# Decoder step: rotary rows of the cache pages by copies to a scratch and one load, instead of gathers

## The chip, the cores and the metric

The kernel runs on one core of a Trainium2 chip. The core has five engines with their own instruction queues: TensorE (PE, matrix products into PSUM), VectorE (DVE), ScalarE (ACT), GpSimd (POOL) and SyncE (SP, which issues DMAs). An engine works through its queue in order; what it needs from another engine or from a DMA it waits for by semaphores. The metric is the device time of one execution in microseconds, median over runs. Less is better.

## The reference, cut to what matters

One layer of a decoder serves 512 prompt rows and 8 samples of 8 new rows each with the same weights. Of the samples' attention this is the part that the change touches: each sample reads 32 cache pages of 128 rows by its page table; a page has latent rows (256 wide) and rotary key rows (32 wide).

```python
def scores(c, kr):
    return (jnp.einsum('bhtl,bkl->bhtk', q_abs, c.astype(f32))
            + jnp.einsum('bhtr,bkr->bhtk', q_r, kr.astype(f32))) * ATTN_SCALE
...
def step(carry, pid):
    m, l, acc = carry
    c = cache_kv_latent[layer, pid]
    kr = cache_k_rope[layer, pid]
    s = scores(c, kr)
    m_new = jnp.maximum(m, jnp.max(s, -1))
    corr = jnp.exp(m - m_new)
    p = jnp.exp(s - m_new[..., None])
    acc = acc * corr[..., None] + jnp.einsum('bhtk,bkl->bhtl', p, c.astype(f32))
    return (m_new, l * corr + jnp.sum(p, -1), acc), None
(m, l, acc), _ = lax.scan(step, (m, l, acc), page_table.T)
```

Around it stand a conditioning (six modulation terms per group of rows), one input projection, causal prompt attention over 8 heads, a short gated convolution, gates, output projection, layer norm, and a SwiGLU feed forward.

## The kernel before

All 576 rows are kept with channels on the partitions, in two halves of 288 columns. A product in full precision is three matmuls of a high and a low part (`mm3`, L117 to L119). A weight tile is loaded by SyncE into `wr` (L107), ScalarE makes the high part `wh` (L57) and VectorE the low part `wl` (L60); there are three `wr` tiles and three pairs of parts.

The program goes through these stages: conditioning and first input tiles; latent projections; the prompt's attention (`prompt_units`), with the convolution units (`fill_conv`, 12 tiles of 48 matmuls) and the rest of the conditioning (`fill_ada`, weights `wa`, two tiles in a ring, L196) as fillers between its parts; the samples' attention (`sample_units`), with gates and projections as fillers; output projection and first norm; feed forward; second norm.

A scheduler that works on a timeline of its own sets the order of each engine's queue from the program. Only on SyncE, and only in the first stage and in the samples' attention, does the order of the program stand (`manual_schedule`).

The samples' attention goes over 4 pairs of samples. For each pair there is one step on the new rows and eight units of four pages for both samples, 32 units in all. `load` fetches a unit two ahead of its use: SyncE reads eight page numbers from `ptab` (L563) into registers and issues eight page loads of 256 KB (L569, tiles `raw`, a ring of 7). GpSimd issues four indirect gathers (L573, tile `kr`, a ring of 3): partition p of a gather gets one row of 128 numbers of `in_krT_dram`, a row number standing in `idx`. So each sample's 32 rotary rows come to 64 partitions, every row twice. In `scores` ScalarE rounds `kr` to `krh` and VectorE makes `krx`, which holds high parts and low parts on different partitions (L625, with the factor `nm`, 0 or -1); two matmuls (L632) multiply it by the queries `qr` after eight on the latent rows (L630). `prepare` makes `qr`, block-diagonal over the two samples.

DMAs of SyncE carry one of eight semaphores in turn (DMAHW0 to DMAHW7 in the order below); one that takes a semaphore waits for the DMA that had it before.

Of the kernel before, what the change touches and what calls it, by code (L numbers as in the profile page):

```python
# [7 lines left out]
F32 = mybir.dt.float32  # L8
# [35 lines left out]
# column offsets of the per-channel vectors  # L44
# [3 lines left out]
def build(tc, a):  # L48
# [29 lines left out]
    psp = pool("psp", space=PSUM)  # L78

# [9 lines left out]
    # ---------------------------------------------------------------- base  # L89
# [6 lines left out]
    # weight stream: pool, ring of split tiles, columns of a tile  # L96
    wp = [pool("w", side="right"), 3, 512, 3]

    def wload(src, n=1024, hl=None, tag="", to=None, eng=None):
        """a weight tile and its exact split, as a list of (hi, lo) pieces of wp[2] columns"""  # L100
# [25 lines left out]
    def gpart(pss, piece, xss, c0, ks, n):  # L126
        """pss[i] += sum over k in ks of piece[:, k-th 128 columns from c0]^T xss[i][k], of n such k in all"""
        for ps, xs in zip(pss, xss):
            for i, k in enumerate(ks):
                c = slice(c0 + 128 * i, c0 + 128 * i + 128)  # L130
                mm3(ps[:, :HT], piece[0][:, c], piece[1][:, c], *xs[k], k == 0, k == n - 1)

    def gemm(pss, w, xss, k0=0):
        """pss[i] = sum over k of w[:, k0+k]^T xss[i][k]; an xs is the (hi, lo) pairs of one half"""
# [4 lines left out]
    def halves(t):  # L139
        """operands of a half-token tile [128, 2, K, HT]"""  # L140
        return [(t[:, 0, k], t[:, 1, k]) for k in range(t.shape[2])]
# [7 lines left out]
    def rsqrt(p, vv, out, table=True):  # L149
        """out = 1/sqrt(vv): exp(-ln/2), then one Newton step"""  # L150
# [15 lines left out]
    # right-hand stack: what outlives the attention phases  # L166
# [10 lines left out]
    idx = keep.tile([128, 4 * NPAGES], I32, name="idx")  # L177
    lane = keep.tile([128, 1], I32, name="lane")
# [7 lines left out]
    # ---------------------------------------------------------------- start: ada, h  # L186
# [31 lines left out]
    # weights of the conditioning, in part where results come later  # L218
# [5 lines left out]
    # a quarter of the conditioning gives a quarter of the modulated rows, and those a quarter of the first three tiles  # L224
# [48 lines left out]
    # ---------------------------------------------------------------- latent projections  # L273
    # on the right what the queries end with, on the left what the prompt's attention ends with
# [88 lines left out]
    # values of the prompt, token-major  # L363
# [9 lines left out]
    # new latent rows of the samples, token-major  # L373
# [8 lines left out]
    dma(out=idx, in_=a["pages_b"])  # L382
    dma(out=lane, in_=a["lane"])
    dma(out=ptab, in_=a["pages"])
    v.tensor_scalar(out=idx, in0=idx, scalar1=32, scalar2=None, op0=MULT)
    tt(idx, idx, lane.to_broadcast([128, 4 * NPAGES]), ADD)
# [4 lines left out]
    # ---------------------------------------------------------------- fillers  # L391
# [70 lines left out]

    def fill_ada():
        for u in range(2, 6):
            yield from ada_mm(u, CV, 2)

    # ---------------------------------------------------------------- prompt attention
    E2 = pool("e2", side="right")
    A2b = pool("a2b")
    # each head's rows of the samples, with the other half's rows zero  # L470
# [25 lines left out]
    def prompt_units():  # L496
        for pr in range(4):
# [32 lines left out]
            for kb in range(4):  # L530
# [9 lines left out]
                # the two heads' columns of the array work side by side  # L540
# [7 lines left out]
    # ---------------------------------------------------------------- sample attention  # L548
    ring = {"raw": (0, NRAW, 5), "kr": (0, 3, 2)}

    def ring_tile(name, shape, dt=F32):
        """the next tile of a ring whose last places are in the later pool"""
# [4 lines left out]
    def load(pa, gg):  # L557
        """GP pages of the two batches, and their rotary rows"""
        pages = {}
        if gg < 0:  # L560
            return pages
        i = pa * NG + gg
        _, vs = nc.values_load_multi_w_load_instructions(  # L563
            ptab[i:i + 1, :], engines=[mybir.EngineType.SP], min_val=0, max_val=n_pool - 1,
            skip_runtime_bounds_check_because="a page table holds indices of the pool")
# [4 lines left out]
        kr = pages["kr"] = ring_tile("kr", [128, GK])  # L570
        for j in range(GP):
            i = pa * NPAGES + GP * gg + j
            g.indirect_dma_start(kr[:, 128 * j:128 * j + 128], None, a["krT"],  # L573
                                 bass.IndirectOffsetOnAxis(ap=idx[:, i:i + 1], axis=0))
        return pages

    def prepare(wk):
        """the samples' queries against latent rows, and the rotary ones"""
# [5 lines left out]
        # rotary queries against [hi, lo] rows of the first batch, then of the second: block-diagonal  # L584
        qf_ = qr.rearrange("p i a e q -> p (i a) e q")
        zero = sel[:, :NS].unsqueeze(1).to_broadcast([128, 8, NS])
        act(qf_[64:128, :, 0], zero[64:128], scale=0.0)
        act(qf_[0:64, :, 1], zero[0:64], scale=0.0)
        ps = ps_sc()
        mm(ps, lhsT=sel, rhs=qsr, start=True, stop=True)  # L590
        for e in range(2):
            src = ps[64 * e:64 * e + 64].rearrange("p (h a e t) -> p e a h t", a=4, e=2, t=NT)[:, e]
            d = qr[64 * e:64 * e + 64].rearrange("p i a e (h t) -> p i e a h t", t=NT)[:, :, e]
# [12 lines left out]
    def sample_units(A3, qa, qr, pages):  # L606
# [6 lines left out]
        def scores(pa, gg, pages):  # L613
            """scores of the step's own rows (gg < 0) or of GP pages"""
# [6 lines left out]
            else:  # L621
                krh = A3.tile([128, GK], F32R, tag="krh", bufs=1, name="krh")
                kx = A3.tile([128, GK], F32R, tag="krx", bufs=2, name="krx")
                act(krh, pages["kr"])
                v.scalar_tensor_tensor(out=kx, in0=krh.bitcast(F32), scalar=nm, in1=pages["kr"], op0=MULT, op1=ADD)  # L625
            # the two batches' columns of the array work side by side
# [565 lines left out]
```

## Time and profile before

| | |
|---|---|
| median of three runs | 1139.51 us (1139.26 to 1141.25) |
| span of the profiled execution | 1174.0 us, granted TensorE clock 0.974 |
| TensorE busy | 1091.8 us, 93% |
| VectorE busy | 537.7 us, 46% |
| ScalarE busy | 431.7 us, 37% |
| GpSimd busy | 225.1 us, 19%; 122.7 us of it the 128 gathers |
| DMA of SyncE's queue | 180.42 MB |
| DMA of GpSimd's queue | 8.40 MB |

The profile is of one execution with the profiler on, whose span is 34.5 us longer than the median of the runs without it. Times in the profile's rows count from the start of that span. Busy time leaves out an engine's waits and, for SyncE, everything: issuing a DMA is not counted as busy, so SyncE is read from its waits and its timeline. A row of waits has the engine and line that waited, what ended the wait, the sum in us, how often, and the longest.

### The profile page before, as it was taken

To read this page: it belongs to the slowest core of one execution; us is meant where nothing else is said; L and a number is where in the kernel's file an instruction comes from. 1 tells how busy PE (TensorE), PEld (TensorE's weight loads), DVE (VectorE), ACT (ScalarE), POOL (GpSimd) and SP (SyncE) were. 2 spreads that over 40 slices of the span, in tenths; PEclk is the share of its full clock that TensorE was granted. 3 is DMA by queue.
4 is the path that set the end of the run, shared out by engine and by line. 5 is a ranking of instruction groups with operands and counts; after the bars stand their busy time and mean duration, and the time that the engine had idled before them with its cause. 6 is when DMAs were issued, how large, how long until landed. Compare 5 with 4: busy or idle time off the path is not lost.

```text
span 1174.0 us, 19868 instructions
## 1 busy us (share of the span) xinstructions
PE 1091.8 (93%) x7646; PEld 931.6 (79%) x7646; DVE 537.7 (46%) x1059; ACT 431.7 (37%) x859; POOL 225.1 (19%) x232
## 2 busy tenths in 40 slices
PE   6889999998798899989999889899999999999994
PEld 5878787785466466556569889899999999999994
DVE  3476354443132333332247787933233333355656
ACT  2474343435232522332346355332223222334433
POOL 1120000023442342441301421800000000001303
PEclk9999999999799998999999899999999999999998
DMA  9626354418389586696675423032222222455551
GB/s 366 209 96 204 122 185 141 140 46 311 106 294 321 170 300 214 220 310 244 203 239 172 159 73 108 3 107 91 90 72 79 100 75 72 118 178 150 157 181 54
DMA packets 84941, 190.07 MB, mean 162 GB/s; under 512 B 11600, under 2 KB 15568, under 8 KB 84848
## 3 DMA queue, kind: packets, MB, share of 16 engines
q1 hardware_dynamic: 80752, 180.42, 45.8%
q0 software_dynamic: 4096, 8.40, 2.3%
q8 instruction: 60, 0.98, 0.3%
q14 instruction: 33, 0.27, 0.1%
HBM read 185.72 MB, written 3.06 MB: 161 GB/s over the span
## 4 chain that ended last, share of the span: by engine, by line
PE 48%; DVE 7%; DMA 5%; issue 2%; ACT 1%; SPq 1%; POOL 0%; POOLq 0%; ACTq 0%; DVEq 0%
PE acc L117 10%; PE acc L118 9%; PE acc L119 9%; PE sc L117 4%; PE sc L119 4%; PE sc L118 4%; PE sc L630 3%; DMA wr<-in_w_ff_dram 3%; PE pv L661 3%; DVE xr L60 2%; DVE wl L60 2%; ACT wh L57 1%; PE sc L632 1%; SPq L569 1%; DMA raw<-in_page_dram 1%
## 5 line engine op out<-in xcount | busy, mean ns | idle before, releaser
L117 PE MATMUL acc<-h,wl 128*128 128x288 f32 x960 | 288.7, 302 | 14.1 <-DVE wl L60 8.5
L118 PE MATMUL acc<-h,wh 128*128 128x288 f32 x960 | 286.9, 299 | 2.0 <-DVE h L60 1.5
L119 PE MATMUL acc<-h,wh 128*128 128x288 f32 x960 | 284.7, 297 | 1.9 <-issue 1.9
L60 DVE TENSOR_TENSOR wl<-wr,wh 128x512 fp32r<-128x512 f32 (+1 forms) x186 | 178.7, 966 | 212.1 <-ACT wh L57 206.1
L57 ACT ACTIVATE wh<-wr 128x512 fp32r<-128x512 f32 (+2 forms) x196 | 156.6, 807 | 194.5 <-DMA wr<-in_w_ff_dram 58.7
L117 PEld LDWEIGHTS acc<-h,wl 128*128 128x128 f32 x960 | 181.5, 189 | 25.9 <-DVE wl L60 11.2
L118 PEld LDWEIGHTS acc<-h,wh 128*128 128x128 f32 x960 | 182.2, 190 | 7.3 <-issue 5.0
L119 PEld LDWEIGHTS acc<-h,wh 128*128 128x128 f32 x960 | 182.6, 190 | 3.1 <-issue 2.9
L573 POOL DMA_INDIRECT kr<-in_krT_dram,idx x128 | 122.7, 959 | 227.4 <-ACT krh L57 103.0
L117 PE MATMUL sc<-h,wl 128*128 128x288 f32 x336 | 99.9, 297 | 0.0
L118 PE MATMUL sc<-h,wh 128*128 128x288 f32 x336 | 99.4, 296 | 0.0
L119 PE MATMUL sc<-h,wh 128*128 128x288 f32 x336 | 99.1, 295 | 0.0
L630 PE MATMUL sc<-raw,qa 128*64 128x512 f32 x256 | 85.3, 634 | 3.2 <-DMA raw<-in_page_dram 1.8
L60 POOL TENSOR_TENSOR xr<-xr,h 128x288 f32<-128x288 f32 x16 | 17.2, 1098 | 366.1 <-ACT h L57 362.5
L117 PE MATMUL acc<-f,wl 128*128 128x288 f32 x288 | 85.9, 298 | 1.6 <-DVE wl L60 1.6
L118 PE MATMUL acc<-f,wh 128*128 128x288 f32 x288 | 84.9, 295 | 0.0
L119 PE MATMUL acc<-f,wh 128*128 128x288 f32 x288 | 84.7, 294 | 0.0
L661 PE MATMUL pv<-raw,pT 128*64 128x256 f32 x512 | 68.8, 401 | 12.5 <-ACT pT L57 6.3
L661 PEld LDWEIGHTS pv<-raw,pT 128*64 128x64 f32 x512 | 38.5, 143 | 37.7 <-issue 16.0
L119 PEld LDWEIGHTS sc<-h,wh 128*128 128x128 f32 x336 | 63.6, 189 | 0.0
L118 PEld LDWEIGHTS sc<-h,wh 128*128 128x128 f32 x336 | 63.3, 189 | 0.1
L117 PEld LDWEIGHTS sc<-h,wl 128*128 128x128 f32 x336 | 63.2, 188 | 0.1
(326 smaller groups left out, 1767.1 us busy)
## 6 DMA issues: line engine op xcount, KB each, us to landing
raw<-in_page_dram SPq DMA_DIRECT2D x256, 256.0 KB
wr<-in_w_ff_dram SPq DMA_DIRECT2D x76, 512.0 KB
wa<-in_w_ada_dram SPq DMA_DIRECT2D x40, 512.0 KB
wr<-in_w_in_dram SPq DMA_DIRECT2D x64, 256.0 KB
wr<-in_w_ff_dram SPq DMA_DIRECT2D x16, 384.0 KB
wr<-in_w_o_dram SPq DMA_DIRECT2D x18, 256.0 KB
wr<-in_w_oa_dram SPq DMA_DIRECT2D x16, 256.0 KB
x<-in_xT_dram SPq DMA_DIRECT2D x4, 576.0 KB
```

The source lines that it names most:

```text
L57: nc.scalar.activation(out=out, in_=in_, func=func, **kw)
L60: return (eng or v).tensor_tensor(out=out, in0=in0, in1=in1, op=op)
L117: mm(ps, lhsT=wl, rhs=xh, start=start, stop=False)
L118: mm(ps, lhsT=wh, rhs=xl, start=False, stop=False)
L119: mm(ps, lhsT=wh, rhs=xh, start=False, stop=stop)
L569: dma(out=raw[:, j], in_=a["page"][bass.ds(vs[GP * e + j], 1)].rearrange("a p d -> p (a d)"))
L573: g.indirect_dma_start(kr[:, 128 * j:128 * j + 128], None, a["krT"], bass.IndirectOffsetOnAxis(ap=idx[:, i:i + 1], axis=0))
L630: mm(ps[rows(e), :n], lhsT=qa[:, c, 2 * pa + e], rhs=rhs, start=c == 0, stop=False)
L632: mm(ps[:, :n], lhsT=qr[:, i, pa].rearrange("p e q -> p (e q)"), rhs=kx, start=False, stop=i == 0)
L661: mm(pv[rows(e), :KVL], lhsT=pT[:np_, j, e], rhs=rhs, start=j == 0, stop=j == nj - 1)
```

## The change

The 128 gathers go, with the tables `idx` and `lane` and the two VectorE instructions that made the row numbers. A scratch `krs` in HBM holds for each of the 32 units 64 rows of 512 numbers: the first sample's 32 rotary rows over four pages, then the second's. A third filler of the prompt's attention, `fill_kr`, writes it: for each unit SyncE reads eight page numbers and issues eight copies from HBM to HBM, each of 32 rows of 128 numbers (16 KB), three units to a convolution unit. In `load` one DMA of SyncE brings a unit's 64 x 512 numbers from the scratch, behind the eight page loads. In `scores` the parts are made by `split`: high parts on partitions 0 to 63, low parts on 64 to 127. `prepare` lays `qr` out to match, by quarters of 32 partitions in place of halves.

```diff
+    krs = pool("kd", space=bass.MemoryType.DRAM).tile([4 * NG, 64, GK], F32, name="krs")
...
+    def fill_kr():
+        for i in range(4 * NG):
+            vs = page_ids(i)
+            for e in range(2):
+                for j in range(GP):
+                    dma(out=krs[i, 32 * e:32 * e + 32, 128 * j:128 * j + 128],
+                        in_=a["krP"][bass.ds(vs[GP * e + j], 1)].rearrange("a r d -> (a r) d"))
+            yield 1
...
-        kr = pages["kr"] = ring_tile("kr", [128, GK])
-        for j in range(GP):
-            i = pa * NPAGES + GP * gg + j
-            g.indirect_dma_start(kr[:, 128 * j:128 * j + 128], None, a["krT"],
-                                 bass.IndirectOffsetOnAxis(ap=idx[:, i:i + 1], axis=0))
+        kr = pages["kr"] = ring_tile("kr", [64, GK])
+        dma(out=kr, in_=krs[i])
...
-        act(qf_[64:128, :, 0], zero[64:128], scale=0.0)
-        act(qf_[0:64, :, 1], zero[0:64], scale=0.0)
         ps = ps_sc()
         mm(ps, lhsT=sel, rhs=qsr, start=True, stop=True)
-        for e in range(2):
-            src = ps[64 * e:64 * e + 64].rearrange("p (h a e t) -> p e a h t", a=4, e=2, t=NT)[:, e]
-            d = qr[64 * e:64 * e + 64].rearrange("p i a e (h t) -> p i e a h t", t=NT)[:, :, e]
+        for r in range(4):
+            e, rr = r % 2, slice(32 * r, 32 * r + 32)
+            act(qf_[rr, :, 1 - e], zero[rr], scale=0.0)
+            src = ps[rr].rearrange("p (h a e t) -> p e a h t", a=4, e=2, t=NT)[:, e]
+            d = qr[rr].rearrange("p i a e (h t) -> p i e a h t", t=NT)[:, :, e]
             act(d[:, 0], src)
             tt(d[:, 1], src, d[:, 0].bitcast(F32), SUB)
...
-                krh = A3.tile([128, GK], F32R, tag="krh", bufs=1, name="krh")
                 kx = A3.tile([128, GK], F32R, tag="krx", bufs=2, name="krx")
-                act(krh, pages["kr"])
-                v.scalar_tensor_tensor(out=kx, in0=krh.bitcast(F32), scalar=nm, in1=pages["kr"], op0=MULT, op1=ADD)
+                split(pages["kr"], kx[0:64], kx[64:128])
...
     def fill_ca():
-        ad = fill_ada()
+        ad, kg = fill_ada(), fill_kr()
         for _ in fill_conv():
             for _ in range(3):
                 next(ad, None)
+                next(kg, None)
             yield 1
```

The change shifts the line numbers by a few: L107 is L108 after it, L196 is L195, L198 is L197, L569 is L578; the copies are L470, the load of `kr` is L580.

SyncE in the prompt's attention, before, near the last convolution units (`wr` are weights of the projections, `wa` of the conditioning):

```order
L107 DMA wr<-in_w_in_dram 128x512 [waits DMAHW7_49,DVE_49]
L196 DMA wa<-in_w_ada_dram 128x1024 [waits DMAHW3_49,PE_49]
L196 DMA wa<-in_w_ada_dram 128x1024 [waits DMAHW5_49,PE_49]
L107 DMA wr<-in_w_in_dram 128x512 [waits DMAHW2_49,DVE_49]
L107 DMA wr<-in_w_in_dram 128x512 [waits DMAHW4_49,DVE_49]
L196 DMA wa<-in_w_ada_dram 128x1024 [waits DMAHW7_49,PE_49]
```

The same queue with the change, one convolution unit. Each copy is a register instruction (ISA) and a DMA; of the eight behind a table read the first and the last are shown:

```order
L108 DMA wr<-in_w_in_dram 128x512 [waits DMAHW2_49,DVE_49]
L195 DMA wa<-in_w_ada_dram 128x1024 [waits DMAHW3_49,PE_49]
L460 TENSOR_LOAD ptab
L470 ISA
L470 DMA krs<-in_krP_dram 32x128 [waits DMAHW4_49]
...
L470 DMA krs<-in_krP_dram 32x128 [waits DMAHW3_49]
L195 DMA wa<-in_w_ada_dram 128x1024 [waits DMAHW4_49,PE_49]
...
L490 DMA wqr<-in_w_uq_dram 128x384 [waits DMAHW6_49]
L108 DMA wr<-in_w_in_dram 128x512 [waits DMAHW7_49,DVE_49]
```

Between two loads of the fillers now stand eight copies and a table read, from the latent projections on to the last convolution unit.

GpSimd before, at the change from the prompt's attention to the samples' (the copies `co` belong to the last convolution unit):

```order
L413 COPY co<-up 128x2 [waits DVE_49]
L414 COPY co<-up 128x16 [waits DVE_49]
L573 DMA kr<-in_krT_dram,idx 128x128 [waits PE_49]
L573 DMA kr<-in_krT_dram,idx 128x128 x3
...
L573 DMA kr<-in_krT_dram,idx 128x128 [waits DMASW4_49,DVE_49]
```

GpSimd with the change, from the same place:

```order
L408 COPY co<-up 128x2 [waits DVE_49]
L409 COPY co<-up 128x16 [waits DVE_49]
L802 TENSOR_SCALAR xr<-xr 128x1152 [waits DMAHW2_49,DMAHW4_49,SP_sequencer_49,DMAHW6_49,DVE_49,PE_49]
L802 TENSOR_SCALAR xr<-xr 128x1152 [waits DMAHW5_49]
L802 TENSOR_SCALAR xr<-xr 128x1152 [waits DMAHW6_49]
```

GpSimd has nothing in the samples' attention; its next work is the residual of the first norm. What it issued stands on SyncE now, the end of a unit's `load`:

```order
L578 DMA raw<-in_page_dram 128x512 [waits DMAHW7_49]
L578 ISA
L578 DMA raw<-in_page_dram 128x512 [waits DMAHW0_49]
L580 DMA kr<-krs 64x512 [waits DMAHW1_49]
L614 DMA smask<-in_smask_dram 128x256 [waits DMAHW2_49,DVE_49]
L108 DMA wr<-in_w_in_dram 128x512 [waits DMAHW3_49]
```

The load of `kr` is behind the unit's last page load and ahead of the next filler weights.

More of the change, by code (lines that the diff above doesn't have):

```diff
@@ L176, in build @@
     ptab = keep.tile([4 * NG, 2 * GP], I32, name="ptab")
-    idx = keep.tile([128, 4 * NPAGES], I32, name="idx")
-    lane = keep.tile([128, 1], I32, name="lane")
     sel = keep.tile([128, 128], F32, name="sel")
@@ L381, in build @@
         split(wukr, wukh[:, c], wukl[:, c], g)
-    dma(out=idx, in_=a["pages_b"])
-    dma(out=lane, in_=a["lane"])
     dma(out=ptab, in_=a["pages"])
-    v.tensor_scalar(out=idx, in0=idx, scalar1=32, scalar2=None, op0=MULT)
-    tt(idx, idx, lane.to_broadcast([128, 4 * NPAGES]), ADD)
     dma(out=mask, in_=a["mask"])
@@ L461, in fill_gates, with page_ids @@
         yield 1
+    def page_ids(i):
+        return nc.values_load_multi_w_load_instructions(
+            ptab[i:i + 1, :], engines=[mybir.EngineType.SP], min_val=0, max_val=n_pool - 1,
+            skip_runtime_bounds_check_because="a page table holds indices of the pool")[1]
+    def fill_kr():
[6 more added lines that the diff above has]
+            yield 1
     def fill_ada():
@@ L562, in load @@
         i = pa * NG + gg
-        _, vs = nc.values_load_multi_w_load_instructions(
-            ptab[i:i + 1, :], engines=[mybir.EngineType.SP], min_val=0, max_val=n_pool - 1,
-            skip_runtime_bounds_check_because="a page table holds indices of the pool")
+        vs = page_ids(i)
         for e in range(2):
@@ L740, in fill_ca @@
                 next(ad, None)
+                next(kg, None)
             yield 1
-        for _ in ad:
-            pass
+        for x in (ad, kg):
+            for _ in x:
+                pass
     def merge(s, f, nf, ns):
@@ L1136, in pack @@
     r["page"] = np.concatenate([ct, ck], 2)
-    r["krT"] = i["cache_k_rope"][0].transpose(0, 2, 1).reshape(-1, PAGE)
+    r["krP"] = i["cache_k_rope"][0].transpose(0, 2, 1)
     pt = i["page_table"]
     r["pages"] = pt.reshape(4, 2, NG, GP).transpose(0, 2, 1, 3).reshape(4 * NG, 2 * GP)
-    r["pages_b"] = np.repeat(pt.reshape(4, 2, NPAGES).transpose(1, 0, 2).reshape(2, -1), 64, 0)
-    r["lane"] = (np.arange(128, dtype=np.int32) % 32)[:, None]
     r["ident"] = np.eye(128, dtype=np.float32)
@@ L1145, in pack @@
     r["sel"] = (p[:, None] % 32 == p[None, :] % 32).astype(np.float32)
-    r["nm"] = np.where(p % 64 < 32, 0.0, -1.0).astype(np.float32)[:, None]
+    r["nm"] = np.where(p < 64, 0.0, -1.0).astype(np.float32)[:, None]
     r["qtab"], r["krtab"] = rope_consts()
```

## The prediction

> **What bounds the kernel now.** I read the stretches first: busy time of each engine between the span's start, the end of the input projections (88), the end of the prompt's attention (256), the start and the end of the samples' attention (300 and 640).
>
> ```profile
> core 0: us, PE busy (x) PEld busy (x) DVE busy (x) ACT busy (x) POOL busy (x), PEclk, DMA share, GB/s
> 60.00:88.00 28.00, 24.50 (x151) 20.76 (x150) 21.58 (x36) 20.31 (x38) 6.27 (x4) 0.94 0.30 98
> 88.00:256.00 168.00, 168.00 (x1212) 134.41 (x1212) 81.29 (x209) 64.04 (x161) 6.85 (x18) 1.00 0.43 145
> 256.00:300.00 44.00, 36.75 (x205) 25.48 (x204) 14.95 (x43) 18.98 (x48) 19.25 (x19) 0.92 0.64 222
> 300.00:640.00 340.00, 313.75 (x1939) 214.15 (x1938) 116.84 (x288) 120.24 (x263) 99.49 (x105) 0.96 0.69 234
> ```
>
> TensorE is the bound: from 88 to 256 it is busy 168.00 of 168 us, from 300 to 640 it is idle for 340 - 313.75 = 26 us. The copies go into the first of these stretches, the gathers leave the last. GpSimd's 99.49 us there are nearly all gathers, on an engine that has time. So the gathers can cost something only where a late one holds TensorE up; the copies cost something where SyncE feeds TensorE late. What SyncE does from 88 to 248 is next: its waits in that window, then the DMAs that it issued in it.
>
> ```profile
> SPq L196 <- PE acc L198: 55.4, 20, 9.0
> SPq L107 <- DVE wl L60: 31.9, 14, 9.3
> SPq L196 <- DMA wa<-in_w_ada_dram: 10.4, 5, 3.8
> SPq L479 <- DVE up L60: 8.1, 1, 8.1
> SPq L479 <- DVE wql L60: 5.6, 3, 2.9
> SPq L107 <- DVE up L60: 4.7, 1, 4.7
> ...
> SPq L479 <- DMA wqr<-in_w_uq_dram: 0.2, 1, 0.2
> ```
> ```profile
> wa<-in_w_ada_dram SPq DMA_DIRECT2D x29, 512.0 KB
> wr<-in_w_in_dram SPq DMA_DIRECT2D x23, 256.0 KB
> wqr<-in_w_uq_dram SPq DMA_DIRECT2D x7, 192.0 KB
> wr<-in_w_ukT_dram SPq DMA_DIRECT2D x2, 256.0 KB
> ```
>
> The six waits shown make 116.1 us and the five others of that answer 6.8, together 122.9 of 160 us. What is left, 37 us, is SyncE's own work for some 62 loads. So SyncE has 123 us to spare there, and that is the room for the copies.
>
> **The price of one copy on SyncE.** No row shows a copy from HBM to HBM, but what an issue costs SyncE is seen.
>
> ```profile
> L569 SPq DMA_DIRECT2D raw<-in_page_dram x256: 3/333/1441, 264.8 to 605.0; - x128
> L569 SPq MOVE raw<-in_page_dram x256: 2/29/723, 264.7 to 604.9; - x128
> L563 SPq TENSOR_LOAD <-ptab x32: 3/536/744, 245.4 to 592.9; - x32
> ```
> ```profile
> 29.17 0.33 SPq L383 DMA_DIRECT2D lane<-in_lane_dram  x1
> 264.82 9.14 SPq L569 DMA_DIRECT2D raw<-in_page_dram  x16
> ```
> ```profile
> raw<-in_page_dram SPq DMA_DIRECT2D x256, 256.0 KB
> ...
> lane<-in_lane_dram SPq DMA_DIRECT2D x1, 0.5 KB
> ```
>
> A page load of 256 KB takes 333 ns to issue, the half KB of `lane` 0.33 us: the size doesn't enter, so a copy of 16 KB costs the same. A copy is addressed through registers as a page load is (FUSED_REGOPS, MOVE, DMA), and 16 of those, with one read of the page table between them, take 9.14 us where nothing holds them up. One unit of eight copies with its table read (0.536 us) is then (9.14 + 0.54) / 2 = 4.84 us; all 32 units are 155 us of SyncE.
>
> A rule speaks against this price. The Trainium skill, page "DMA: Bandwidth & Descriptors", section "Issuing engines are not separate DMA queues", says that the sequencer's time to initiate a DMA is usually small relative to the DMA itself. For transfers this small the rows above say otherwise; by the rule the copies would cost nothing, the sum below would be 1.5 - 2 = -0.5 us, and with the gathers' gain at its end it is rival 2.
>
> **Where the copies stand.** The order of SyncE (shown with the change) decides what they hold up. Loads that followed each other directly now have eight copies between them, 24 in a convolution unit, up to the last one. SyncE works in order, so the weights of the next unit leave only after all 24. Of the 256 copies 48 stand ahead of 88 us (by the place of the loads around them), 208, or 26 units, behind.
>
> **The sum.**
> 1. Copies in the prompt's attention. 37 + 26 x 4.84 = 163 us of SyncE in a stretch of 160: +3 us even if every wait of today goes. TensorE has no idle time in this stretch that could take it, and its own work stays.
> 2. Waits of SyncE that stay. A wait for TensorE to release a conditioning tile averages 55.4 / 20 = 2.8 us and has 4.84 us of copies ahead of it: covered. The longest, 9.0, leaves 4.2. Behind such a wait stand the next copies and the next unit's weights, for which ACT, DVE and then TensorE wait. I take two of these, +8 us; ends 0 and 31.9 (the weight loads' wait for DVE staying whole).
> 3. Landing. Each DMA of SyncE waits for the one eight places earlier (DMAHW0 to DMAHW7 go round in the order shown), so a copy that lands later than eight issues, 8 x (9.14 - 0.54) / 16 = 4.3 us, slows the queue. The nearest landing is a gather's beside page loads:
>
> ```profile
> 413.37 0.94 POOL kr L573
> 414.31 0.30 issue
> 414.62 4.67 DMA kr<-in_krT_dram,idx
> 419.29 0.03 issue
> 419.37 0.48 issue
> 419.84 0.74 DVE krx L625
> ```
>
> At 4.67 us each group of eight would take 0.37 longer, 26 x 0.37 = 10 us. I take 0, because the prompt's stretch moves 145 GB/s and this place was in one of 234; ends 0 and 10. The same page of the Trainium skill, "Anatomy of one DMA", puts the fixed part of a DMA at about 2 us with HBM the slowest target, by which this item is 0; no row here shows a write to HBM landing.
> 4. The 48 early copies: 6 x 4.84 = 29 us before 88 us, where SyncE waits mostly for DVE and TensorE. I take 0, ends 0 and +4 (one group of copies ahead of a query weight).
> 5. The queries' preparation: zero fills and casts go by quarters, twice as many instructions.
>
> ```profile
> 264.27 1.27 ACT L57 ACTIVATE qr<-sel 64x512 fp32r<-64x512 f32 x2
> 265.56 0.38 ACT L57 ACTIVATE qr<-sc 64x256 fp32r<-64x256 f32 x1
> PE sc L536 <- ACT qa L57: 0.5, 1, 0.5
> ```
>
> Width sets the time, so ACT gets 1.27 + 2 x 0.38 = 2.0 us more, right where TensorE waited for ACT's qa. I take +1.5; ends +0.5 and +2.
> 6. The gathers go. At most: the 413 us place (0.94 + 0.30 + 4.67 = 5.9) and TensorE's 2.12 us before the first rotary product,
>
> ```profile
> 280.21 0.60 ACT L57 ACTIVATE oh<-pv 128x512 fp32r<-128x512 f32 x1 [2.95 <-PE pv L543]
> 281.44 0.74 DVE L625 SCALAR_TENSOR_TENSOR krx<-krh,nm,kr 128x512 fp32r<-128x512 f32 x1
> 282.24 0.73 PE L632 MATMUL sc<-krx,qr 128*128 128x512 f32 x2 [2.12 <-issue]
> ```
>
> 8 us. But TensorE had other matmuls at 413, and at 280 ACT and DVE came to kr only behind the end of the prompt's attention (oh), which itself waited for TensorE. In return the load of kr is issued on SyncE behind eight page loads: 0.5 us later than the pages at most, and SyncE has room there. -2; ends -8 and +5 (ten late units at 0.5).
> 7. ACT and DVE on kr: still one pass each over 512 columns, and the tables idx and lane leave the start: 0, under cover of TensorE.
>
> Sum: 3 + 8 + 0 + 0 + 1.5 - 2 + 0 = +10.5 us. The profiled execution (1174.0) would become 1184.5; it is 34.5 above the median of the three runs, 1139.51, and I put the same difference on that: 1150.0.
>
> **Rivals.**
> 1. *Slower by much*: copies land late or more of SyncE's waits survive, and the prompt's attention goes at the pace of SyncE. Items 2 and 3 at their ends give +10.5 + 10 = +20.5 to +10.5 + 10 + 23.9 = +44.4, 1160 to 1184; I take 1172. For it: copies and weights alternate to the end, and a late copy holds weights. Against: short waits are covered.
> 2. *Faster*: SyncE's spare time takes the copies and the gathers' late places go. The place is the stretch from 88 to 248 and the point is a unit's price: with two long waits staying, (160 - 37 - 8) / 26 = 4.4 us; below it copies are free. The price here is 4.84, of which the part between records may be the profiler's own. Then 1.5 - 8 = -6.5: 1133. The rule of the Trainium skill cited above would end here.
> 3. *No change*: copies just fit and the rest cancels (0 + 1.5 - 2 = -0.5): 1139. It needs a unit between 4.4 and 4.6 us.
>
> **How the numbers follow.** Chances: forecast 0.60 (1150, its own range 1142 to 1163, from item 2 at 0 to items 2 and 3 at half), rival 1 0.14, rival 2 0.17, rival 3 0.09. A measurement of this kernel tells 0.2%, 2.3 us, from no change. So faster 0.17, same 0.09, slower 0.60 + 0.14 = 0.74. The range runs from 1134, most of rival 2, to 1178, half of rival 1.
>
> **What the profile after would show.** SyncE's waits for TensorE and DVE from 88 to 248 shrink from 87 us to under 20, while 256 copies appear at about 0.33 us each, 0.54 apart. TensorE, ACT or DVE wait for wr<-in_w_in, and TensorE is no longer busy all the time from 88 on; the first page load leaves at about 276 instead of 264.82. Waits of SyncE for copies to land would speak for rival 1. From the first page load to the end little changes, TensorE's idle time from 300 to 640 stays near 26 us. The forecast is wrong if SyncE still waits 40 us or more in the prompt's attention with TensorE full (rival 2), or if the stretch grows beyond 30 us (rival 1).

## The result, and the profile after

The changed kernel takes 1199.55 us (median of 4 runs, 1196.03 to 1202.26), the kernel before 1140.38 (4 runs, 1139.26 to 1141.58): 1.0509 times as long, interval 1.0479 to 1.0540, +59 us. The direction was forecast, the size (+10.5, at most +38) was not.

The kernel before has two levels, by chip, 1140 to 1145 us on the chip of this comparison and on one later, 1173 to 1178 us on three others (its profiled execution of 1174.0 is of that kind), while the changed kernel takes 1197 to 1200 us on all three chips where it ran. So each ratio below is taken against runs of the kernel before on the same chip.

The stretches of the changed kernel, as those of before were shown:

```profile
core 0: us, PE busy (x) PEld busy (x) DVE busy (x) ACT busy (x) POOL busy (x), PEclk, DMA share, GB/s
60.00:88.00 28.00, 23.69 (x131) 20.72 (x129) 19.72 (x33) 18.56 (x37) 5.89 (x4) 0.88 0.35 110
88.00:256.00 168.00, 136.33 (x906) 107.45 (x905) 65.24 (x171) 51.43 (x129) 1.70 (x12) 0.90 0.38 121
256.00:300.00 44.00, 35.18 (x244) 28.64 (x246) 15.90 (x37) 12.01 (x30) 0.33 (x2) 0.88 0.49 160
300.00:640.00 340.00, 324.36 (x2069) 224.66 (x2062) 122.18 (x299) 130.53 (x297) 0.00 (x0) 0.99 0.76 245
```

TensorE was busy for all of 88 to 256; now it is idle for 32 of these 168 us, does 906 matmuls instead of 1212, and its granted clock falls to 0.90. The loss is there. The copies, and the page loads in the same form (duration of one in ns, least, median and longest):

```profile
L470 SPq MOVE krs<-in_krP_dram x256: 29/29/38, 37.3 to 285.3; - x128
L470 SPq DMA_DIRECT2D krs<-in_krP_dram x256: 492/492/1424, 37.3 to 285.4; - x128
DMA to landing us min/median/max: 1.8/2.0/4.8
...
L578 SPq DMA_DIRECT2D raw<-in_page_dram x256: 332/333/1217, 318.2 to 620.0; - x128
```

A copy of 16 KB costs SyncE 492 ns, a page load of 256 KB 333. The first page load leaves at 318.2 us instead of 264.8: 53 us later, nearly the whole loss. SyncE's order of work late in the prompt's attention, and its waits from 88 to 248 us (four more rows are under half a microsecond each):

```profile
230.63 5.24 SPq L470 DMA_DIRECT2D krs<-in_krP_dram  x8
235.97 0.53 SPq L195 DMA_DIRECT2D wa<-in_w_ada_dram  x1
237.27 11.23 SPq L470 DMA_DIRECT2D krs<-in_krP_dram  x16
248.59 1.00 SPq L108 DMA_DIRECT2D wr<-in_w_in_dram  x2
```
```profile
SPq L195 <- PE acc L197: 7.6, 6, 4.4
SPq L195 <- PE sc L120: 1.7, 4, 0.7
SPq L108 <- DVE S L538: 0.7, 2, 0.4
```

Sixteen copies take 11.23 us, eight 5.24, so one more unit with its table read is 11.23 - 5.24 = 5.99 us, not 4.84. SyncE's waits have shrunk from 123 us to 11: it works nearly all the time, and what it has to load waits behind the copies. Weights come between blocks of 8 and 16 copies. The loads pay too: directly behind a copy a weight load takes 0.53 us to issue (second row), where the half KB of `lane` and the conditioning weights of the kernel before (median) took 0.33.

On the chip of the later comparison there are traces of both kernels, 1143.4 us before and 1198.6 after, with first page loads at 263.9 and 315.9 us. TensorE's waits in the changed kernel there from 88 to 318 us:

```profile
PE sc L118 <- DVE wql L60: 19.9, 5, 6.0
PE acc L197 <- DMA wa<-in_w_ada_dram: 13.2, 5, 4.5
PE sc L547 <- DVE S L538: 3.3, 2, 1.7
```

`wql` is the split of a query weight, `wa` a conditioning weight: both are loads that stand behind copies. All idle time of TensorE in this stretch is 39.9 us (19 pauses, summed from the records), where the kernel before has 0.4 us from 88 us to its first page load. Ahead of the first page load both kernels do the same 1891 matmuls, in 247.1 us of busy time before and 259.9 after. So of the 52 us 39 are idle time and 13 are matmuls that take longer. The windows around two such pauses show the lower clock (TensorE idle from 200.5 to 206.5, and again from 225.0 to 229.0):

```profile
core 0: us, PE busy (x) PEld busy (x) DVE busy (x) ACT busy (x) POOL busy (x), PEclk, DMA share, GB/s
190.00:200.00 10.00, 9.33 (x62) 5.95 (x65) 0.80 (x2) 2.69 (x7) 0.00 (x0) 1.00 0.21 65
206.60:210.00 3.40, 3.40 (x14) 3.40 (x15) 1.47 (x3) 1.03 (x2) 0.00 (x0) 0.50 0.55 196
210.00:213.00 3.00, 3.00 (x20) 3.00 (x19) 1.41 (x3) 1.03 (x3) 0.00 (x0) 0.79 0.38 72
213.00:216.00 3.00, 3.00 (x25) 3.00 (x24) 0.12 (x1) 0.00 (x0) 0.00 (x0) 1.00 0.37 141
...
228.90:232.00 3.10, 2.96 (x12) 2.96 (x13) 1.01 (x3) 0.98 (x2) 0.00 (x0) 0.50 0.65 228
232.00:236.00 4.00, 4.00 (x18) 2.91 (x17) 1.98 (x4) 1.14 (x3) 0.00 (x0) 0.60 0.38 111
```

After the pause of 6 us the clock stands at 0.50 for some 5 us, so such a pause costs more than its length.

Behind the first page load little is lost: 879.5 us to the end before (1143.4 - 263.9), 882.7 after (1198.6 - 315.9).

### The profile page after: what moved, and what is told of

It is laid out like the page before. It is cut to its first block, busy times and chain, and to the rows that moved or that the text cites. A ratio compares the mean times of both kernels' runs of the same rounds, so it can differ in the third digit from the quotient of the medians.

```text
span 1194.2 us, 20436 instructions
## 1 busy us (share of the span) xinstructions
PE 1089.9 (91%) x7646; PEld 938.7 (79%) x7646; DVE 541.4 (45%) x1059; ACT 435.2 (36%) x863; POOL 101.2 (8%) x104
## 4 chain that ended last, share of the span: by engine, by line
PE 70%; DMA 10%; DVE 7%; SPq 6%; ACT 3%; issue 3%; POOL 1%; POOLq 0%; ACTq 0%; DVEq 0%
PE acc L118 13%; PE acc L119 13%; PE acc L120 13%; PE sc L634 5%; PE sc L118 5%; PE sc L119 5%; PE sc L120 5%; PE pv L665 4%; SPq L470 4%; DMA wr<-in_w_ff_dram 3%; DMA kr<-krs 2%; DVE xr L60 2%; DVE wl L60 2%; DMA raw<-in_page_dram 2%; PE sc L636 1%
## 5 line engine op out<-in xcount | busy, mean ns | idle before, releaser
L634 PE MATMUL sc<-raw,qa 128*64 128x512 f32 x256 | 79.0, 604 | 2.1 <-DMA raw<-in_page_dram 1.8
L60 DVE TENSOR_TENSOR s<-s,sc 128x288 f32<-128x288 f32 x44 | 19.9, 453 | 80.8 <-PE sc L120 80.8
L118 PEld LDWEIGHTS acc<-f,wl 128*128 128x128 f32 x288 | 54.0, 188 | 1.5 <-DVE wl L60 0.8
```

The costliest lines, as they stand in the source:

```text
L60: return (eng or v).tensor_tensor(out=out, in0=in0, in1=in1, op=op)
L118: mm(ps, lhsT=wl, rhs=xh, start=start, stop=False)
L634: mm(ps[rows(e), :n], lhsT=qa[:, c, 2 * pa + e], rhs=rhs, start=c == 0, stop=False)
```

## The experiments

Spans from the profiled execution of each kernel, split at the first page load; the ratio and its interval are of the timed runs, against the kernel before on the same chip.

| kernel | before there, us | time, us | ratio | first page load | from there to the end |
|---|---|---|---|---|---|
| before, chip as in the result | 1144.99 | 1145.13 | | 263.9 | 879.5 |
| before, chip of e1 to e3 (e0 again) | 1178.42 | 1181.69 | | 263.6 | 916.3 |
| before, another chip | 1176.77 | 1179.03 | | 263.9 | 913.4 |
| after, chip as in the result (a2) | 1144.99 | 1199.88 | 1.049 [1.0451, 1.0528] | 315.9 | 882.7 |
| after, chip of the result | 1140.38 | 1199.55 | 1.0509 [1.0479, 1.0540] | 318.2 | 876.0 |
| after, another chip (a1) | 1176.77 | 1196.86 | 1.0161 [1.0117, 1.0205] | 318.5 | 881.6 |
| e1 one copy a unit | 1178.42 | 1160.72 | 0.9843 [0.9779, 0.9907] | 278.1 | 879.8 |
| e2 fixed pages | 1178.42 | 1177.50 | 0.9984 [0.9953, 1.0014] | 297.3 | 881.5 |
| e3 copies on GpSimd | 1178.42 | 1169.68 | 0.9925 [0.9899, 0.9951] | 267.7 | 901.0 |
| e4 direct small loads, SyncE | 1176.77 | 1203.89 | 1.0230 [1.0185, 1.0275] | 263.4 | 938.2 |
| e5 alternate queues | 1176.77 | 1188.14 | 1.0086 [1.0050, 1.0123] | 299.8 | 886.1 |
| e6 copies alone | 1173.45 | 1220.02 | 1.0387 [1.0350, 1.0425] | 315.4 | 900.2 |
| e7 no copies, no gathers | 1173.45 | 1147.21 | 0.9771 [0.9734, 0.9808] | 263.7 | 878.3 |
| e8 small loads, GpSimd | 1173.45 | 1139.73 | 0.9717 [0.9676, 0.9758] | 263.6 | 873.6 |
| e8 again, chip as in the result | 1144.99 | 1140.93 | 0.9967 [0.9947, 0.9988] | 264.0 | 875.2 |
| e9 more gathers, chip as in the result | 1144.99 | 1153.59 | 1.0084 [1.0057, 1.0111] | 263.9 | 884.9 |

**The theory** is that SyncE's time to issue the copies, in order ahead of the prompt's weights, is the whole loss. **The rivals**: the traffic of 4 MB read and 4 MB written; the other order that TensorE, ACT and DVE got; a loss in the samples' attention.

**Before once more.**

> The kernel before, unchanged, for a second profiled execution, because the first one (1174.0 us) was 34.5 us above the time of its runs. All theories: about 1140 us, and a span near the time; the first page load at 264 to 266 us as in the first profile, so that the 34 us are missing behind it, in the samples' attention or later. If instead the first page load comes earlier than 264, the comparison of the two traces up to there (53.4 us lost) was wrong as well.

1181.69 us, beside 19 other runs of 1171.96 to 1185.28, so not 1140: a chip on which the kernel before is slower, as in its first profile. The first page load is at 263.6, and the difference lies behind it, as expected.

**One copy a unit.**

```diff
-            vs = page_ids(i)
-            for e in range(2):
-                for j in range(GP):
-                    dma(out=krs[i, 32 * e:32 * e + 32, 128 * j:128 * j + 128],
-                        in_=a["krP"][bass.ds(vs[GP * e + j], 1)]...)
+            dma(out=krs[i], in_=a["krP"][8 * i:8 * i + 8]...)
```

> The changed kernel with one copy of 128 KB for a unit in place of eight copies of 16 KB and the table read: 32 copies in all, the same 4 MB into the same scratch at the same places of the program, the consuming side unchanged. It leaves out the choice of the pages by the table and the layout, so the rotary rows are not the reference's. Theory (SyncE's issue time is the cost): 32 copies of some 0.5 us are 16 us, well within the 123 us that SyncE had to spare; the time falls back to 1134 to 1146 us, the first page load to 264 to 268 us. Rival 'traffic' (4 MB read and written in HBM slow the weights down): the bytes are the same, so about 1190 to 1200. Rival 'order' (the other order of work on TensorE, ACT and DVE, and the load of kr behind the page loads) would leave a remainder of some 10 to 40 us above 1140, to be seen behind the first page load.

18 us faster than the kernel before, with the same bytes moved, so the bytes alone do not explain the loss. The time is outside the 1134 to 1146 us expected: from the first page load on, this version is some 36 us faster than the kernel before on this chip (879.8 against 916.3), but that load came at 278.1, not at 264 to 268. Without the table read the copies stood in blocks early on in SyncE's order of work:

```profile
35.28 13.27 SPq L467 DMA_DIRECT2D krs<-in_krP_dram  x19
48.67 0.98 SPq L108 DMA_DIRECT2D wr<-in_w_in_dram  x2
49.70 7.44 SPq L467 DMA_DIRECT2D krs<-in_krP_dram  x12
```

Two weight loads stand behind 13 us of copies and the next ones behind 21, and TensorE was busy for 19.8 of the 28 us from 60 to 88 (24.5 before). All copies left before 57 us, so this run does not say what copies do as traffic beside the later weights; the next but one bears on that.

**Fixed pages.**

```diff
-            vs = page_ids(i)
...
-                        in_=a["krP"][bass.ds(vs[GP * e + j], 1)].rearrange("a r d -> (a r) d"))
+                        in_=a["krP"][8 * i + GP * e + j])
```

> The changed kernel with all 256 copies of 16 KB, from fixed page numbers: no read of the page table and no register arithmetic ahead of a copy. It leaves out the choice of the pages for the rotary rows. Theory (issue time): a copy then costs its 0.49 us and little beside it, 0.50 to 0.55 apart in place of 0.68, and the table read of 0.54 a unit goes; 26 units become 26 x (8 x 0.15 + 0.54) = 45 us shorter on SyncE, so about 1150 to 1165 us. Rival 'traffic': same bytes and same number of copies, 1190 to 1200. If copies without registers take 0.33 us each, the register form is what made them dearer than a page load, and the time falls to 1140.

A miss in the price (the copies' row, then two blocks of SyncE's order of work):

```profile
L469 SPq DMA_DIRECT2D krs<-in_krP_dram x256: 488/588/1970, 33.4 to 264.2; - x128
```
```profile
222.57 9.98 SPq L469 DMA_DIRECT2D krs<-in_krP_dram  x16
...
234.18 4.93 SPq L469 DMA_DIRECT2D krs<-in_krP_dram  x8
```

A unit is 9.98 - 4.93 = 5.05 us instead of 5.99; the table read (0.54) explains more than half of the difference, and registers little. Copies without registers take longer to issue, 588 ns, and are still some 0.63 us apart ((4.93 - 0.49) / 7). The first page load moves 21 us forward against the changed kernel, half of what was expected, and the time, 1177.50, is outside the 1150 to 1165 us; the direction fits the theory, and by traffic nothing should have moved.

**Copies on GpSimd.**

```diff
-            vs = page_ids(i)
+            vs = page_ids(i, mybir.EngineType.Pool)
...
-                    dma(out=krs[...
+                    g.dma_start(out=krs[...
```

> The changed kernel with the 256 copies and their table reads issued by GpSimd, which has little to do up to 286 us, in place of SyncE. Nothing is left out. Theory (issue time on SyncE, ahead of the prompt's weights): SyncE gets its spare time back, 1133 to 1146 us, first page load at 264 to 270 us, SyncE's waits for TensorE in the prompt's attention back at some 85 us. Rival 'traffic': the same copies in the same stretch, 1190 to 1200. If a copy costs GpSimd more than 1 us, the last ones end behind 290 us and the loads of kr wait for them: then a loss shows behind the first page load only.

The same 256 copies from the same table, on the other queue: SyncE's waits for conditioning tiles come back and the first page load with them. A wait of SyncE from 88 to 250 us, the copies, and two waits of TensorE, from 0 to 90 and from 250 to 330 us:

```profile
SPq L195 <- PE acc L197: 53.1, 16, 9.0
```
```profile
L470 POOL DMA_DIRECT2D krs<-in_krP_dram x256: 497/497/742, 37.6 to 261.4; - x128
```
```profile
PE acc L118 <- ACT h L57: 10.4, 3, 8.6
```
```profile
PE acc L118 <- DVE cs L60: 9.4, 1, 9.4
```

It beats the kernel before on its chip by 0.75%, but the time expected (1133 to 1146 us) is missed: from the first page load on it stays 23 us behind what e7 shows to be possible (901.0 against 878.3). Part of this is the same mechanism on the other queue. GpSimd's first 14 copies stand ahead of its own instruction on the rows `hf`, at 46.36 us instead of 41.51 in e7, and the next stands behind ten more, at 52.87 us; TensorE waits 8.6 us for what ACT makes of them (third row; 1.5 in e7). Only 1819 of the 1891 matmuls stand ahead of the first page load here, so that load comes early for the work done, and some of the loss shows behind it. A wait of 9.4 us at the end of the prompt's attention is seen too (fourth row). What these leave, which may be traffic, was not followed up.

**The changed kernel and the kernel before on another chip.**

> The changed kernel once more, because the kernel before took 1178 us on the chip of the first four experiments and 1140 us beside the first run of the changed kernel: the two parts of its loss (copies, and the samples' side) must be read on one chip. Theory (issue time): on the chip with 1178 us the loss is 20 to 30 us only (1195 to 1205), because one copy a unit was 18 us faster there than the kernel before, and the eight copies cost 35 to 45; where the kernel before takes 1140 us the loss is again 55 to 62. Rival 'chip' (the other chip is 3% slower at everything): the ratio stays at 1.05, 1235 us beside 1178.

> The kernel before, a third profiled execution. If its time is near 1140 us: TensorE's pauses without a releaser from 260 to 700 us (18 to 20 us in the two traces so far) are gone or far fewer, since this is where the two executions of 1174 and 1180 us could have lost; GpSimd's gathers take 0.94 us each as before. If it is near 1178 us: the same pauses again.

+20 us there, as the theory had it, and not 1235: only the kernel before is slower on that chip. Its third trace has the pauses of TensorE again (below).

**Direct small loads.**

```diff
-            vs = page_ids(i)
-            for e in range(2):
...
             yield 1
...
-        dma(out=kr, in_=krs[i])
+        for e in range(2):
+            for j in range(GP):
+                dma(out=kr[32 * e:32 * e + 32, 128 * j:128 * j + 128],
+                    in_=a["krP"][bass.ds(vs[GP * e + j], 1)]...)
```

> No scratch: SyncE loads the eight rotary tiles of 16 KB of a unit straight into its tile in SBUF, behind the unit's eight page loads, with the same registers; nothing copied in the prompt's attention. Nothing is left out. It prices the same transfer with another destination. If the destination (HBM) made a copy dear: 0.33 us each, 0.54 apart. If the small size or its 32 rows do: 0.49 us, 0.68 apart. Time by the theory of issue time: in the samples' attention SyncE then has 32 x (0.54 + 8 x 0.54 + 8 x 0.54) = 294 us, and some 20 us of other loads, in about 335 us: just enough at 0.54 apart, 0 to 15 us slower than one copy a unit (0.985 to 0.998 of the kernel before where that takes 1178 us); at 0.68 apart it is 330 us and SyncE bounds the stretch, 15 to 35 us slower. The first page load goes back to 264 to 280 us in either case.

The small loads, a block of them in SyncE's order of work, and a wait of SyncE from 300 to 640 us:

```profile
L577 SPq DMA_DIRECT2D kr<-in_krP_dram x256: 315/316/1250, 268.1 to 628.5; - x128
```
```profile
400.01 4.07 SPq L577 DMA_DIRECT2D kr<-in_krP_dram  x8
```
```profile
SPq L577 <- DMA raw<-in_page_dram: 32.9, 106, 1.9
```

This settles that neither the small size nor the 32 rows nor the register address makes a copy dear: with all three a load into SBUF costs 316 ns, (4.07 - 0.32) / 7 = 0.54 us apart, as the prediction had priced the copies; the copy from HBM to HBM costs 492. Why is not shown. A destination in HBM is not dear by itself: the kernel before stores `out_krope` from SBUF to HBM in 0.34 to 0.35 us. Nor is every load into SBUF cheap: the one load of 128 KB a unit takes 451 ns from the scratch, and 474 from the input in e7. The time is a miss: from 300 to 640 us TensorE is idle for 46 us and waits for page loads (14.2) and for `kr` (6.9), so SyncE limits the stretch even at that price. Third row: 106 times SyncE waited for an earlier page load to land before it could issue, the mechanism of the prediction's item 3, which did not show for copies that land in 2.0 us but does beside page loads.

**Alternate queues.**

```diff
+            on_g = i % 2
-            vs = page_ids(i)
+            vs = page_ids(i, mybir.EngineType.Pool if on_g else mybir.EngineType.SP)
...
-                    dma(out=krs[...
+                    (g.dma_start if on_g else dma)(out=krs[...
```

> The changed kernel with every second unit's copies (16 of 32) and their table reads issued by GpSimd, the others by SyncE. Nothing is left out. Theory (issue time): SyncE's part is 13 units x 5.9 = 77 us in the prompt's attention, below the 123 us that it had to spare, GpSimd's 16 x 8 x 0.87 = 111 us over 220 us; so no loss on either side, the time of one copy a unit (0.98 to 0.988 of the kernel before where that takes 1178 us), the first page load at 264 to 280 us. Rival 'traffic': the same 256 copies, so the time of the changed kernel.

A miss that says where copies hurt (SyncE's order of work from 49.77 us on, and a wait of TensorE from 30 to 300 us):

```profile
49.77 22.40 SPq L471 DMA_DIRECT2D krs<-in_krP_dram  x30
72.27 0.53 SPq L324 DMA_DIRECT2D krt<-in_krtab_dram  x1
```
```profile
PE sc L316 <- DVE sq L60: 15.0, 1, 15.0
```

The scheduler put all of SyncE's copies ahead of 163 us, thirty in one block before the small table `krt`, which left at 45.94 us in the kernel before. TensorE lost its time between 60 and 120 us instead (busy for 32 of these 60 us); from 120 to 270 it was busy throughout. The first page load is 36 us late with 128 copies on SyncE, 53 with 256 in the changed kernel: half the copies cost more than half, so the count alone does not decide.

**Copies alone.** The kernel before with the change's `fill_kr` put in at the same place, gathers kept, the scratch unread.

```diff
+    krs = pool("kd", space=bass.MemoryType.DRAM).tile([4 * NG, 64, GK], F32, name="krs")
...
-        ad = fill_ada()
+        ad, kg = fill_ada(), fill_kr()
```

> The kernel before, gathers and all, with the change's 256 copies, table reads and register reads on SyncE put in at the same places, into a scratch that nobody reads. The copies are pure extra work. Theory (SyncE's issue time ahead of the weights): the first page load leaves at 312 to 322 us as in the changed kernel, and the time grows by 45 to 62 us over the kernel before on the same chip, whichever chip it is (1.038 to 1.053). Rival 'order' (the loss up to the first page load comes from the other order of TensorE, ACT and DVE in the changed kernel): first page load before 290 us, time up by less than 25 us.

+46.6 us and the first page load at 315.4. Both are as expected by the theory. The copies by themselves make the loss; the other order of the changed kernel is not needed for it.

**No copies, no gathers.**

```diff
-        dma(out=kr, in_=krs[i])
+        dma(out=kr, in_=a["krP"][8 * i:8 * i + 8]...)
```

> The changed kernel without any copy: SyncE loads a contiguous 128 KB for a unit's rotary rows straight from the pool, one load a unit; the choice of the pages for the rotary rows is left out. It prices the gathers: the samples' side of the change alone. First page load at 262 to 266 us. Where the kernel before takes 1177 us (three traces with 18 to 20 us of TensorE's pauses without a releaser, which are gone in every kernel without gathers): 1138 to 1150 us, that is 0.967 to 0.977 of it. Where it takes 1140 us: 1135 to 1145, no difference, and then the gathers cost nothing on that chip. Rival 'the pauses don't matter' (the first page load is all that counts): 1170 to 1180 where the kernel before takes 1177.

1147.21 us, 26 us faster than the kernel before on this chip: there the samples' side without gathers gains, and it is the other half of the account: 1176.8 - 31.8 (913.4 to 881.6 behind the first page load) + 54.6 (263.9 to 318.5) = 1199.6, against 1196.9 measured for the changed kernel on such a chip.

**Small loads by GpSimd.** e4 with the loads and a table read of its own on GpSimd.

```diff
+        vg = page_ids(i, mybir.EngineType.Pool)
...
+                g.dma_start(out=kr[32 * e:32 * e + 32, 128 * j:128 * j + 128],
+                            in_=a["krP"][bass.ds(vg[GP * e + j], 1)]...)
```

> No scratch and no indirect gathers: GpSimd reads the unit's row of the page table into registers and issues eight plain loads of 16 KB straight into the unit's tile, where it issued four indirect gathers before; SyncE issues the page loads only. Nothing is left out. GpSimd needs about 8 x 0.87 + 0.5 = 7.5 us for a unit, and a unit takes 10 us: it keeps up. If the indirect gathers themselves made TensorE's pauses (their descriptors, written row by row), the pauses are gone and the time is that of e7 within 8 us: 0.967 to 0.982 where the kernel before takes 1177 us. If any traffic on GpSimd's queue beside the page loads makes them, they stay, 0.99 to 1.0.

> The plain loads by GpSimd again, on another chip: 1136 to 1146 us as before. Where the kernel before takes 1177 us, 0.967 to 0.976 of it; where it takes 1140, 0.997 to 1.005, and the gathers cost nothing there.

```profile
302.89 4.53 POOL L578 DMA_DIRECT2D kr<-in_krP_dram  x8 [0.79 <-issue]
310.56 4.53 POOL L578 DMA_DIRECT2D kr<-in_krP_dram  x8 [3.15 <-DVE sm L60]
```

A unit takes GpSimd 4.53 us plus the table read, where the four gathers took 4 x 0.94 plus 0.30 between them; GpSimd has room. The rows are of the second chip, GpSimd in order of time. This version takes 0.9717 and 0.9967 of the kernel before on the two chips where it ran, the second gain a small one of 0.3%, and at 1140 us it is below the 1197 to 1200 of the changed kernel.

**What the gathers do.** The kernel before on a chip where it takes 1177 us, TensorE and GpSimd (in brackets idle time before the instruction, and what ended it; "issue": nothing that the profile shows):

```profile
294.04 0.39 PE L118 MATMUL acc<-h,wh 128*128 128x288 f32 x1 [0.77 <-issue]
294.08 0.95 POOL L573 DMA_INDIRECT kr<-in_krT_dram,idx  x1 [0.30 <-issue]
...
295.34 0.94 POOL L573 DMA_INDIRECT kr<-in_krT_dram,idx  x1 [0.31 <-issue]
295.46 0.27 PE L653 MATMUL sc<-ident,S 128*128 128x128 f32 x1 [0.41 <-issue]
...
296.58 0.95 POOL L573 DMA_INDIRECT kr<-in_krT_dram,idx  x1 [0.30 <-issue]
297.58 0.37 PE L653 MATMUL sc<-ident,S 128*128 128x128 f32 x1 [0.98 <-issue]
```

In step with the gathers TensorE pauses. Such pauses sum to 16 to 20 us in the four traces with gathers on the chips of that kind; of the 19.8 us in this one 17.6 lie within a gather or the microsecond behind it, and these cover 57% of the stretch from 280 to 572 us. On the same three chips the kernels without gathers (e1, e2, e3, e4, e5, e7, e8, a1) have 0 to 1.7 us. To see whether gathers alone make them:

> The changed kernel again, for a chip on which the kernel before takes 1140 us, if this one is such. All theories: 1194 to 1203 us, as on both chips so far, with the first page load at 318 us; the kernel before beside it takes either 1173 to 1180 us (ratio 1.016) or 1140 (1.05).

> The kernel before with a profile. At 1173 to 1182 us: 16 to 20 us of TensorE's pauses without a releaser from 260 us on, in step with the gathers. At 1140 us: the gathers there, the pauses not.

> The kernel before, with the four gathers of every second unit made twice, into the same place: 192 instead of 128, nothing else changed. If each gather holds TensorE up (the pauses stand in step with them, 1.24 us apart at 292 to 300 us): 64 / 128 x 18 to 20 = 9 to 10 us more pauses, and with the lower clock behind them 9 to 18 us in all, 1.008 to 1.015 of the kernel before. Rival (the pauses are something else that falls into the same stretch; GpSimd has time for 64 more gathers of 1.24 us): within 4 us, 0.997 to 1.003.

The chip turned out to be of the kind of the result. There the same gathers run (0.94 us each, 128 of them), TensorE has no such pause over 0.15 us and the kernel before takes 1145; so the pauses were seen only with gathers, but gathers alone do not make them. Behind the first page load the chips differ by 33.9 us (913.4 against 879.5); 19.8 of these are the pauses, and the granted clock from 300 to 640 us is 0.96 against 0.98. That the pauses make the rest as well is not shown. `e9_more_gathers` (four gathers twice in every second unit) did land in its expected range, but for another reason:

```profile
PE pv L661 <- ACT pT L57: 9.6, 5, 6.2
```

No pauses, but waits of TensorE for ACT from 256 to 640 us, 9.6 us against 1.8 in the kernel before on this chip. It therefore says nothing of the pauses, and why they go with the gathers on some chips stays open.

## Why the prediction was right or wrong

*The direction and the mechanism* were right: SyncE's spare time is used up by the copies, the weights behind them come late, and TensorE, busy all the time before, waits. The signs named came: waits of SyncE for TensorE and DVE from 87 us to about 11, waits of ACT for `wr<-in_w_in` of 28.7 us (none before), TensorE no longer full from 88 on. So did the sign that the forecast is wrong: the stretch grew by 52 us, beyond the 30 that the prediction allowed.

*Item 1 failed, in its price.* "The size doesn't enter, so a copy of 16 KB costs the same": the two rows compared (256 KB and half a KB) both went from HBM to SBUF. Size indeed does not enter there (16 KB in e4: 316 ns), but the copy goes from HBM to HBM and costs 492 ns, and a unit 5.99 us instead of 4.84. The item's own sum becomes 37 + 26 x 5.99 = 193 us in 160: +33 instead of +3. With the 8 us of waits that stay (item 2, about right: 11 were seen) that makes 41 us, against the 38 by which the last copy, at 286 us, ends behind the old end of the stretch at 248. Rival 2's deciding point, 4.4 us a unit, was further off than the 0.44 us that the prediction saw.

*What the sum left out* is what follows from late weights: the last of the weights `in_w_in` ahead of the samples' attention leaves at 295 us (at 224 in the kernel before on that chip), so the work behind them is done after that, and the longer pauses of TensorE are followed by a lower clock. Taken by TensorE instead of SyncE, the 52 us are 39 us idle and 13 us at the lower clock. No term of the sum stood for either. A sum by the queue that is late gives when it ends; the cost is what the engine behind it does from then on.

*Item 3 was right*: the copies land in 2.0 us (1.8 to 4.8), and no wait of SyncE for one is listed; 0 was the value taken. The 2 us cited with this item stand in the Trainium skill for DMAs that GpSimd issues; these copies, issued by SyncE, took as long. *Item 4* (early copies free) was right for this order, TensorE 23.7 of 28 us busy against 24.5 from 60 to 88; e5 and e1 show that it hung on how the scheduler spread them.

*Items 5 to 7* sum to -0.5 us and were nearly right on a chip like that of the result: behind the first page load 879.5 before, 882.7 after. On chips like that of the profile they were wrong by 32 us (913.4 to 881.6), for there TensorE pauses beside the gathers. The profile showed this: rows of waits of TensorE on "issue" in the samples' attention. The prediction took the 34.5 us between the profiled execution and the median as something that both kernels would share ("I put the same difference on that"), though only one of them has gathers. On such a chip the change costs 20 us (1.0161), twice the 10.5 forecast: dearer copies, less the loss that goes with the gathers.

*TensorE's idle time from 300 to 640* was to stay near 26 us; it is 15.6. The 26 were of the execution with pauses; the kernel before without them has 340 - 323.8 = 16.

*The rivals.* Rival 1 was nearest in size (1160 to 1184), and the prompt's attention does go at the pace of SyncE, as it said; but neither late landings nor more of SyncE's waits, which it named as the reasons, were seen; the price of a copy and the clock brought the time beyond it. Rival 2, by the Trainium skill, page "DMA: Bandwidth & Descriptors", section "Issuing engines are not separate DMA queues": that spreading DMAs over engines saves only the sequencer's time to initiate them agrees with e3 and e8; that this time is usually small relative to the DMA itself does not make it small in sum here, where a copy takes 0.49 us to issue and 2.0 us to land, and 256 of them cost 46.6 us (e6).

## What to carry to other kernels

Price an issue from a row of the same kind of transfer, source and destination both, and where none exists, measure one: 0.49 us against the assumed 0.33 mis-sized this forecast. A queue with spare time on average can still not take in small DMAs if they stand ahead of weights that the bound engine needs in order; put them on a queue where nothing urgent stands behind (in e3 GpSimd's own `hf` still did), and load straight to the place of use, without the scratch (e8 does both; the same loads on SyncE, e4, made it 2.3% slower than the kernel before). When a profile and the timed runs differ by more than the spread of the runs, find out what the profile's execution has that the other has not, before the difference is carried to another kernel.

## What the runs showed of the hardware that was not expected

- SyncE's issue of a DMA from HBM to SBUF: 0.33 us for half a KB (`lane`) and 256 KB (`raw`), 0.32 for 16 KB (e4), but 0.45 us for the 128 KB of `kr` from the scratch, 0.47 for the same tile from the input (e7), and 0.53 for a weight load directly behind a copy. From HBM to HBM it takes 0.49 us with a register address and 0.59 without, for 16 KB (e2: 0.588) as for 128 KB (e1: 0.587).
- TensorE's granted clock falls to 0.50 in pauses of 4 to 6 us and stays there for some 5 to 6 us once the matmuls go on (the windows above). The Trainium skill, page "TensorE: Matmul & The Clock Gate", section "Part 1: The HAM clock gate (the "warmup" mystery)", says that the clock halves after an idle window of about 3.4 us and comes back after a busy one; the trace agrees with the halving, and shows the return later than one such window of work, at some 5 and 6 us.
- On the chips where the kernel before takes 1173 to 1178 us, the gathers go with pauses of TensorE, and SyncE is hit too: its register moves ahead of page loads range from 2 to 720 ns there, and from 29 to 37 ns on the chip where it takes 1145 us (the kernel before on the one, then on the other). Without gathers they range from 29 to 38 ns on the first kind of chip too (a1, e1, e7).

```profile
L569 SPq MOVE raw<-in_page_dram x256: 2/29/720, 263.9 to 602.2; - x128
```
```profile
L569 SPq MOVE raw<-in_page_dram x256: 29/29/37, 263.8 to 570.8; - x128
```
